# Layer 0 of a two-layer encoder: four k tiles of the query and key projection moved into the first two pieces of the input projection, running sums reloaded into PSUM

## The chip, the cores and the metric

The kernel runs on one NeuronCore of a Trainium2 chip. Its engines work side by side, each on its own queue in order: PE (TensorE, matmuls), DVE (VectorE), ACT (ScalarE), POOL (GpSimd) and SP (SyncE, which here issues nearly all transfers). They meet through semaphores. The metric is the device time of one execution in microseconds, the median of several runs.

## What is computed

A trunk of two layers over 256 positions of width 2048. Each layer makes a conditioned, normalised input h, projects it once with a wide matrix, feeds the columns to four mixers, projects back, and adds a gated feed-forward network:

```python
for l in range(DEPTH):
    mod = (c_act @ w_mod[l] + b_mod[l]).reshape(bn, 6, d)
    ...
    h = layer_norm(x) * (1.0 + scale_m) + shift_m
    proj = h @ w_in[l]
    uv, q_c, kv_c, k_r, sb, sc, sh, ag = jnp.split(proj, IN_SPLITS, axis=-1)
    y_a = gmlp_mixer(uv, ...)
    y_b = mla_mixer(q_c, kv_c, k_r, ...)
    y_c = short_conv_mixer(sb, sc, sh, sconv_w[l])
    y_d = conformer_conv(ag, ...)
    y = jnp.concatenate([y_a, y_b, y_c, y_d], axis=-1) @ w_out[l]
    x = layer_norm(ALPHA * x + (1.0 + gate_m) * y, post_mix_g[l], post_mix_b[l])
    h = layer_norm(x) * (1.0 + scale_f) + shift_f
    x = layer_norm(ALPHA * x + (1.0 + gate_f) * conv_ffn(h, ...), post_ffn_g[l], post_ffn_b[l])
```

All is float32. The modulation `mod` of both layers needs 2 x 2048 x 12288 weights, about 200 MB, for a single vector c.

## The kernel before

**Modulation.** It runs on DVE: each step multiplies a 128-row stripe of `w_mod` (tile `wmod`, one transfer of about 1 MB into one of four raw buffers) by a scalar per partition and adds it to an accumulator (`qacc` for layer 0's first two vectors, `macc` for the rest). A product on PE with a column of ones (`ps_mod`) then sums over partitions. The steps beyond the first two vectors come from a generator, `mods`: `pump` draws from it at a rate per unit of weights, set by the stage (`RATES`), and `STEPS` says how many queued background pieces of the convolution (`convD` taps, a product on ACT and an add on DVE) each unit releases.

**Layer 0's input projection, by pieces.** The first h depends on shift and scale, which take 33 MB of `w_mod`. So `by_pieces` cuts the 16 k tiles of the contraction into five pieces (`PIECES`: 2, 2, 4, 4, 4 tiles). While piece q is multiplied, the modulation columns of piece q + 1 are streamed in, in the shares that `some_mods` names. In each piece the columns of four groups are multiplied in four steps s: a quarter of group D (1024 columns, kept in four PSUM banks throughout), then in `side` one of the groups U, V and E (512 columns, two banks). Six banks of this kind (`acc_tile`) exist, so U, V and E share the two that D leaves. After each piece `side` evacuates them: ACT copies a bank, DVE adds it to a running sum in SBUF (lines 1284 to 1290).

**Two kinds of weights.** In the first four k tiles (`PLAIN_KT`), and for U, V and E up to the last piece, weights are used as plain float32 (`exact`, tile `wexact`); one such product is two rows on PE in the profile. Elsewhere a weight tile `wraw` is split into a high part (`whi`, a cast on ACT) and the rest (`wlo`, a subtraction on DVE), three products each. Exact tiles take the buffers of `whi` and `wlo` in turn, four each, so eight in rotation.

**Behind the pieces** come `mix_d` (starts the convolution: `gluD`), `mix_u` (GELU of U's sums), `mix_v`, then stage B, the 768 columns of query, key-value and rotary key over all 16 k tiles (`group`, eight units of two tiles, all exact, banks `B_c`), with `mix_b` (attention, `kvr` to `yb`) flushed into stage C, the last group of columns; then the output projection. `stream` runs each unit's products one unit after its load.

**Order.** Instructions go to each engine's queue in an order that a scheduler sets at build time; a queue never overtakes. All transfers of weights and of `w_mod` stand in SP's one queue, so that a transfer whose buffer is still in use holds all those behind it.

Of the kernel before, what the change touches and what calls it, by code (L numbers as in the profile page):

```python
# [13 lines left out]
P = 128  # L14
# [18 lines left out]


RATES = [
    dict(B=1.6, C=1.9, out=1.7, first=1.2, up=0.68, down=0.83),
    dict(D=0.8, U=0, V=0, B=0.3, C=0.6, E=0.6, out=0.6, up=0.3, down=0.7),
]

STEPS = [  # L40
    dict(B=2, C=2, up=2),
    dict(U=5, V=5, B=4, C=6, E=6, up=2),
]

# [10 lines left out]
def encoder_kernel(ctx: ExitStack, tc: tile.TileContext, A: dict, consts: bass.AP, out: bass.AP):  # L55
# [23 lines left out]
    def acc_tile(name):  # L79
        return accp.tile([P, 512], F32, tag="acc", name=name)  # L80

    def mm(o, lhsT, rhs, start, stop):
        pe.matmul(o, lhsT, rhs, start=start, stop=stop, skip_group_check=True)  # L83
# [389 lines left out]
        act.copy(hi, src)  # L473
        dve.tensor_tensor(out=lo, in0=src, in1=hi.bitcast(F32), op=ALU.subtract)  # L474

    def group(w, c0, width, name, then, ntm=0, nk=2, hF=None, bg=0, spare=0):

        ncm = (width - 512 * ntm) // P  # L480
        box = {}

        def products(item, u):
            if u == 0:
                box["c"] = [acc_tile(f"{name}_c{i}") for i in range((ncm + 1) // 2)]
                box["t"] = [[acc_tile(f"{name}_t{t}{i}") for i in range(ntm)] for t in range(2)]
                box["h"] = list(hT)
            for part in (range(0, min(4, ncm)), range(4, ncm)):
# [33 lines left out]
        def end():  # L522
            then(box["c"], box["t"])

        return KT // nk, load, products, end, bg

    def group2(w, c0, name, then, bg=0, spare=0):


        nk = 4  # L530
        box = {}

        def products(item, u):
            if u == 0:
                box["c"] = [acc_tile(f"{name}_c{i}") for i in range(4)]
                box["h"] = list(hT)
            for i in range(4):
                for k, (hi, _) in enumerate(item):
                    kt = u * nk + k
                    both = box["h"][kt // 2][2][:, kt % 2, :, :].rearrange("p h t -> p (h t)")  # L540
                    mm(box["c"][i], hi[:, i * P : (i + 1) * P], both, kt == 0, False)
            for i in range(4):
                for k, (_, lo) in enumerate(item):
                    kt = u * nk + k
                    high = box["h"][kt // 2][0][:, kt % 2, :]
                    mm(box["c"][i][:, :S], lo[:, i * P : (i + 1) * P], high, False, kt == KT - 1)

        def load(u):
            return weights(w, u * nk, nk, c0, 512, False, spare if u == 0 else 0)

        return KT // nk, load, products, lambda: then(box["c"]), bg

    def run(g):
        units, load, products, end, bg = g
        for u in range(units):
            stream(lambda: load(u), lambda item, u=u: products(item, u), bg)
        pending.append(end)

# [684 lines left out]
    def by_pieces(l, w_in, hF, between, mix_d, mix_u, mix_v, mix_b, mix_c, mix_e):  # L1243
# [1 line left out]

        hf = lambda kt: hF[kt // 4][:, kt % 4, :]
        accD = [acc_tile(f"D{l}_c{i}") for i in range(4)]
        cols = {"U": C_UV, "V": C_UV + 512, "E": C_SB}

        hT[:] = [None] * (PLAIN_KT // 2) + [act_pair("hT") for _ in range((KT - PLAIN_KT) // 2)]  # L1250
        sums = {}
# [17 lines left out]
                    mm(o, w[:, i * P : (i + 1) * P], x, first and n == 0 and i % 2 == 0, last and n == len(ts) - 1)  # L1269

        def side(g, parts, k0, nkt):
            ps = [acc_tile(f"{g}{l}_{i}") for i in range(2)]
            for kt, part in parts:
                st, sp = kt == k0, kt == k0 + nkt - 1
                if g == "V":
                    ts = terms(kt, part)
                    for t in range(2):
                        for n, (w, x) in enumerate(ts):
                            mm(ps[t], x[:, t * P : (t + 1) * P], w, st and n == 0, sp and n == len(ts) - 1)
                else:  # L1280
                    chan_major(ps, kt, part, range(4), st, sp)
            for i in range(2):
                if k0 == 0:
                    act.copy(sums[g][i], ps[i])
                elif k0 + nkt == KT:
                    dve.tensor_tensor(out=sums[g][i], in0=ps[i], in1=sums[g][i], op=ALU.add)
                else:
                    part = tmp_tile("part")
                    act.copy(part, ps[i])
                    dve.tensor_tensor(out=sums[g][i], in0=part, in1=sums[g][i], op=ALU.add)  # L1290

        first = between(0)[1]
        first()
        for q, (k0, nkt) in enumerate(PIECES):
# [3 lines left out]

            def load(g, kt):

                c0, width = (C_AG, 1024) if g == "D" else (cols[g], 512)
                nk = min(2048 // width, nkt)
                for j, p in enumerate(weights(w_in, kt, nk, c0, width, exact or (g != "D" and q < len(PIECES) - 1))):
                    loaded[(g, kt + j)] = p

# [14 lines left out]
            for s in range(4):  # L1320
# [5 lines left out]
                    ahead[1]()  # L1326
                for kt, h in mine:
                    d_part(kt, h)
                if s < 3:
                    g = "UVE"[s]  # L1330
                    load(g, k0)
                    some_mods((0.5, 0.85, 1.0)[s])
                    side(g, [(kt, loaded[(g, kt)]) for kt in range(k0, k0 + nkt)], k0, nkt)
        mix_d(accD, None)
        mix_u(sums["U"], None)
        mix_v(None, [[x] for x in sums["V"]])
        phase(l, "B")
        run(group(w_in, C_Q, 768, f"B{l}", mix_b, hF=hf, bg=STEPS[l]["B"]))
        phase(l, "C")

        def mix_ce(cps, tps):
# [265 lines left out]
```

## Time and profile before

| what | value |
|---|---|
| median of 3 runs | 2297.42 us (2294.97 to 2298.74) |
| the profiled execution's own time | 2298.88 us |
| its span, first to last instruction | 2297.1 us, mean granted PE clock 0.987 |
| PE busy | 2238.4 us, 97% |
| DVE busy | 1790.7 us, 78% |
| ACT busy | 1071.6 us, 47% |
| moved | 605.21 MB, mean 263 GB/s |

The profile is of one execution. Busy shares are means over stages with different limits, so the views used below cut the span into stretches: layer 0's pieces lie between 29.6 and 188.6 us, stage B up to 235.5, stage C and attention up to 327, where the output projection starts. A row of the timeline merges instructions of one kind: start, length, engine, line, operation, output <- inputs, shapes and count, and in brackets the idle time before it with its releaser. On SP the length is that of issuing, waits included, not that of the transfer.

### The profile page before, as it was taken

The numbers are of one execution on the slowest core, as the hardware profiler recorded it, in microseconds if no ns is written. First come the engines' busy times: TensorE is split into PE (matmuls) and PEld (weight loads), VectorE is DVE, ScalarE is ACT, GpSimd is POOL, SyncE is SP. The second block draws the span as 40 slices with busy tenths as digits, with TensorE's granted clock in tenths as the row PEclk, the third lists the DMA queues.
The fourth block names the chain that finished last, engine by engine and source line by source line (L and its number), as shares of the span: only waits on it lengthen the run. The fifth ranks groups of instructions, "written<-read, shape, count | busy, mean of one in ns | idle before, by whom it ended". The sixth has DMA issues, their size and how long they took to land.

```text
span 2297.1 us, 31478 instructions
## 1 busy us (share of the span) xinstructions
PE 2238.4 (97%) x12387; PEld 1934.1 (84%) x12387; DVE 1790.7 (78%) x2211; ACT 1071.6 (47%) x1597; POOL 34.4 (1%) x65
## 2 busy tenths in 40 slices
PE   6899999999999999999999999999999999999998
PEld 4688886798888888888789999889888888888886
DVE  6878987778888888998977899796676565565676
ACT  2235742335454544544455435545454454454553
POOL 2000000000000000000000000000000000000000
PEclk9899999999999999999999999999999999999999
DMA  9999788777889888898857677875665555555554
GB/s 344 362 340 343 271 321 333 263 278 279 317 303 335 292 326 318 303 354 307 311 186 260 202 238 252 291 260 185 249 243 202 193 178 197 192 193 185 188 195 147
DMA packets 228717, 605.21 MB, mean 263 GB/s; under 512 B 14660, under 2 KB 27188, under 8 KB 210900
## 3 DMA queue, kind: packets, MB, share of 16 engines
q1 hardware_dynamic: 227784, 602.30, 73.7%
q8 instruction: 97, 1.59, 0.3%
q0 software_dynamic: 784, 0.90, 0.1%
q14 instruction: 52, 0.43, 0.0%
HBM read 601.05 MB, written 2.10 MB: 263 GB/s over the span
## 4 chain that ended last, share of the span: by engine, by line
PE 89%; DVE 5%; DMA 3%; issue 1%; ACT 1%; SPq 0%; POOL 0%; DVEq 0%; POOLq 0%; ACTq 0%
PE g_c L83 21%; PE v_c L83 21%; PE d L83 20%; PE o L83 8%; PE D_c L83 4%; PE C_c L83 4%; PE B_c L83 3%; DMA wmod<-in_w_mod_dram 2%; PE U_c L83 1%; DVE wlo L454 1%; PE U L83 1%; PE E L83 1%; PE ps_mod L83 1%; PE E_c L83 1%; DVE qacc L248 1%
## 5 line engine op out<-in xcount | busy, mean ns | idle before, releaser
L453 ACT CAST whi<-wraw 128x1024 fp32r<-128x1024 f32 (+1 forms) x632 | 643.6, 1043 | 780.4 <-PE g_c L83 210.0
L454 DVE TENSOR_TENSOR wlo<-wraw,whi 128x1024 fp32r<-128x1024 f32 (+1 forms) x632 | 750.6, 1214 | 292.2 <-ACT whi L453 278.3
L83 PE MATMUL d<-whi,a 128*128 128x512 f32 x1344 | 390.6, 392 | 0.9 <-ACT whi L453 0.9
L248 DVE SCALAR_TENSOR_TENSOR macc<-wmod,cact,macc 128x2048 f32<-128x2048 f32 (+2 forms) x174 | 353.8, 2033 | 32.3 <-DMA wmod<-in_w_mod_dram 31.7
L83 PE MATMUL v_c<-hT,whi 128*128 128x512 f32 (+1 forms) x1456 | 343.1, 383 | 0.0
L83 PE MATMUL g_c<-hT,whi 128*128 128x512 f32 (+1 forms) x1344 | 313.3, 380 | 0.0
L83 PEld LDWEIGHTS v_c<-hT,whi 128*128 128x128 f32 x1456 | 264.6, 189 | 48.5
L83 PEld LDWEIGHTS d<-whi,a 128*128 128x128 f32 x1344 | 253.2, 189 | 54.6 <-ACT whi L453 2.2
L83 PEld LDWEIGHTS g_c<-hT,whi 128*128 128x128 f32 x1344 | 243.4, 189 | 43.2
L83 PE MATMUL d<-wlo,a 128*128 128x512 f32 x672 | 234.4, 392 | 1.6 <-DVE wlo L454 1.6
L83 PE MATMUL v_c<-hT,wlo 128*128 128x256 f32 x1400 | 190.7, 283 | 0.0
L83 PEld LDWEIGHTS v_c<-hT,wlo 128*128 128x128 f32 x1400 | 183.1, 191 | 6.6
L83 PE MATMUL g_c<-hT,wlo 128*128 128x256 f32 x1280 | 175.8, 283 | 0.0
L83 PEld LDWEIGHTS g_c<-hT,wlo 128*128 128x128 f32 x1280 | 168.2, 191 | 5.9
L83 PEld LDWEIGHTS d<-wlo,a 128*128 128x128 f32 x672 | 127.0, 189 | 30.3 <-DVE wlo L454 3.9
L473 ACT CAST a<-g 128x512 fp32r<-128x512 f32 x132 | 80.8, 619 | 91.0 <-PE d L83 89.3
L83 PE MATMUL o<-whi,a 128*128 128x512 f32 x384 | 112.4, 398 | 0.8 <-ACT whi L453 0.8
L474 DVE TENSOR_TENSOR a<-g,a 128x512 fp32r<-128x512 f32 x132 | 87.7, 685 | 9.5 <-ACT a L473 9.5
L83 PEld LDWEIGHTS o<-whi,a 128*128 128x128 f32 x384 | 73.1, 191 | 17.5 <-ACT whi L453 1.2
L83 PE MATMUL D_c<-hT,whi 128*128 128x256 f32 x432 | 82.0, 290 | 2.8 <-ACT hT L473 2.3
L248 DVE SCALAR_TENSOR_TENSOR qacc<-wmod,cact,qacc 128x1024 f32<-128x1024 f32 (+1 forms) x75 | 80.3, 1070 | 2.6 <-DMA wmod<-in_w_mod_dram 0.5
L1364 DVE SCALAR_TENSOR_TENSOR u<-g,pf,u 128x254 f32<-128x254 f32 (+1 forms) x176 | 73.5, 476 | 3.0 <-ACT u L86 3.0
(371 smaller groups left out, 2603.7 us busy)
## 6 DMA issues: line engine op xcount, KB each, us to landing
wraw<-in_ffn_w_up_dram SPq DMA_DIRECT2D x168, 1024.0 KB, 5.0
wmod<-in_w_mod_dram SPq DMA_DIRECT2D x134, 1024.0 KB, 6.2
wraw<-in_ffn_w_down_dram SPq DMA_DIRECT2D x88, 1024.0 KB, 5.2
wraw<-in_w_in_dram SPq DMA_DIRECT2D x33, 1024.0 KB, 6.9
wmod<-in_w_mod_dram SPq DMA_DIRECT2D x64, 512.0 KB, 9.2
wraw<-in_w_out_dram SPq DMA_DIRECT2D x26, 1024.0 KB, 6.7
wmod<-in_w_mod_dram SPq DMA_DIRECT2D x32, 768.0 KB, 6.6
wexact<-in_w_in_dram SPq DMA_DIRECT2D x46, 512.0 KB, 7.4
```

What stands on the lines that cost most here:

```text
L83: pe.matmul(o, lhsT, rhs, start=start, stop=stop, skip_group_check=True)
L248: i = dve.scalar_tensor_tensor(out=acc, in0=w, scalar=col, in1=acc, op0=ALU.mult, op1=ALU.add)
L453: act.copy(hi[:, :m], r)
L454: i = dve.tensor_tensor(out=lo[:, :m], in0=r, in1=hi[:, :m].bitcast(F32), op=ALU.subtract)
L473: act.copy(hi, src)
L474: dve.tensor_tensor(out=lo, in0=src, in1=hi.bitcast(F32), op=ALU.subtract)
L1364: dve.scalar_tensor_tensor(out=u[:, sh:], in0=x[:, : S - sh], scalar=col(k, j), in1=u[:, sh:], op0=ALU.mult, op1=ALU.add)
```

## The change

- Group B joins the two exact pieces: step s = 1 now runs V and then B (768 columns, three banks one after the other). Its sums lie in two new slots, `sumB0` and `sumB1`. Stage B's `group` starts at k tile 4 (`begun`): its first products find the three sums copied into its banks by ACT.
- `side` works one bank at a time. From the second piece on ACT first copies the running sum back into the bank, the products add to it, and ACT copies the bank out. The adds on DVE are gone.
- In the last piece U's two banks are not copied out: `mix_u` reads them at once, in that step, and no longer behind `mix_d`.
- Three steps of `mods` are drawn in the last piece, one after each of its first three steps. Stage B's rate is 1.634 instead of 1.6 over six units instead of eight, and it releases three background pieces a unit instead of two.

```diff
@@ -33,12 +33,12 @@
 
 
 RATES = [
-    dict(B=1.6, C=1.9, out=1.7, first=1.2, up=0.68, down=0.83),
+    dict(B=1.634, C=1.9, out=1.7, first=1.2, up=0.68, down=0.83),
     dict(D=0.8, U=0, V=0, B=0.3, C=0.6, E=0.6, out=0.6, up=0.3, down=0.7),
 ]
 
 STEPS = [
-    dict(B=2, C=2, up=2),
+    dict(B=3, C=2, up=2),
     dict(U=5, V=5, B=4, C=6, E=6, up=2),
 ]
 
@@ -473,16 +473,21 @@
         act.copy(hi, src)
         dve.tensor_tensor(out=lo, in0=src, in1=hi.bitcast(F32), op=ALU.subtract)
 
-    def group(w, c0, width, name, then, ntm=0, nk=2, hF=None, bg=0, spare=0):
+    def group(w, c0, width, name, then, ntm=0, nk=2, hF=None, bg=0, spare=0, begun=None):
 
 
 
         ncm = (width - 512 * ntm) // P
         box = {}
 
+        skip = 0 if begun is None else PLAIN_KT // nk
+
         def products(item, u):
-            if u == 0:
+            if u == skip:
                 box["c"] = [acc_tile(f"{name}_c{i}") for i in range((ncm + 1) // 2)]
+                if begun is not None:
+                    for bank, part in zip(box["c"], begun):
+                        act.copy(bank, part)
                 box["t"] = [[acc_tile(f"{name}_t{t}{i}") for i in range(ntm)] for t in range(2)]
                 box["h"] = list(hT)
             for part in (range(0, min(4, ncm)), range(4, ncm)):
@@ -522,7 +527,7 @@
         def end():
             then(box["c"], box["t"])
 
-        return KT // nk, load, products, end, bg
+        return range(skip, KT // nk), load, products, end, bg
 
     def group2(w, c0, name, then, bg=0, spare=0):
 
@@ -548,11 +553,11 @@
         def load(u):
             return weights(w, u * nk, nk, c0, 512, False, spare if u == 0 else 0)
 
-        return KT // nk, load, products, lambda: then(box["c"]), bg
+        return range(KT // nk), load, products, lambda: then(box["c"]), bg
 
     def run(g):
         units, load, products, end, bg = g
-        for u in range(units):
+        for u in units:
             stream(lambda: load(u), lambda item, u=u: products(item, u), bg)
         pending.append(end)
 
@@ -1245,7 +1250,7 @@
 
         hf = lambda kt: hF[kt // 4][:, kt % 4, :]
         accD = [acc_tile(f"D{l}_c{i}") for i in range(4)]
-        cols = {"U": C_UV, "V": C_UV + 512, "E": C_SB}
+        cols = {"U": (C_UV, 512), "V": (C_UV + 512, 512), "E": (C_SB, 512), "B": (C_Q, 768)}
 
         hT[:] = [None] * (PLAIN_KT // 2) + [act_pair("hT") for _ in range((KT - PLAIN_KT) // 2)]
         sums = {}
@@ -1269,26 +1274,28 @@
                     mm(o, w[:, i * P : (i + 1) * P], x, first and n == 0 and i % 2 == 0, last and n == len(ts) - 1)
 
         def side(g, parts, k0, nkt):
-            ps = [acc_tile(f"{g}{l}_{i}") for i in range(2)]
-            for kt, part in parts:
-                st, sp = kt == k0, kt == k0 + nkt - 1
-                if g == "V":
-                    ts = terms(kt, part)
-                    for t in range(2):
+            for i, total in enumerate(sums[g]):
+                o = acc_tile(f"{g}{l}_{i}")
+                if k0 > 0:
+                    act.copy(o, total)
+                for kt, part in parts:
+                    st, sp = kt == 0, kt == k0 + nkt - 1
+                    if g == "V":
+                        ts = terms(kt, part)
                         for n, (w, x) in enumerate(ts):
-                            mm(ps[t], x[:, t * P : (t + 1) * P], w, st and n == 0, sp and n == len(ts) - 1)
+                            mm(o, x[:, i * P : (i + 1) * P], w, st and n == 0, sp and n == len(ts) - 1)
+                    else:
+                        chan_major([None] * i + [o], kt, part, (2 * i, 2 * i + 1), st, sp)
+                if g == "U" and k0 + nkt == KT:
+                    u_banks.append(o)
                 else:
-                    chan_major(ps, kt, part, range(4), st, sp)
-            for i in range(2):
-                if k0 == 0:
-                    act.copy(sums[g][i], ps[i])
-                elif k0 + nkt == KT:
-                    dve.tensor_tensor(out=sums[g][i], in0=ps[i], in1=sums[g][i], op=ALU.add)
-                else:
-                    part = tmp_tile("part")
-                    act.copy(part, ps[i])
-                    dve.tensor_tensor(out=sums[g][i], in0=part, in1=sums[g][i], op=ALU.add)
-
+                    act.copy(total, o)
+            if u_banks and g == "U":
+                mix_u(u_banks, None)
+
+        u_banks = []
+        both = [slot("sumB0"), slot("sumB1")]
+        sums["B"] = [both[i // 2][:, (i % 2) * 512 : (i % 2 + 1) * 512] for i in range(3)]
         first = between(0)[1]
         first()
         for q, (k0, nkt) in enumerate(PIECES):
@@ -1298,8 +1305,8 @@
 
             def load(g, kt):
 
-                c0, width = (C_AG, 1024) if g == "D" else (cols[g], 512)
-                nk = min(2048 // width, nkt)
+                c0, width = (C_AG, 1024) if g == "D" else cols[g]
+                nk = min(max(2, 2048 // width), nkt) if exact else min(2048 // width, nkt)
                 for j, p in enumerate(weights(w_in, kt, nk, c0, width, exact or (g != "D" and q < len(PIECES) - 1))):
                     loaded[(g, kt + j)] = p
 
@@ -1326,16 +1333,16 @@
                     ahead[1]()
                 for kt, h in mine:
                     d_part(kt, h)
-                if s < 3:
-                    g = "UVE"[s]
+                for g in ("U", "VB", "E", "")[s] if exact else ("U", "V", "E", "")[s]:
                     load(g, k0)
-                    some_mods((0.5, 0.85, 1.0)[s])
+                    some_mods((0.5, 0.85, 1.0, 1.0)[s])
                     side(g, [(kt, loaded[(g, kt)]) for kt in range(k0, k0 + nkt)], k0, nkt)
+                if k0 + nkt == KT and s < 3:
+                    next(mods)
         mix_d(accD, None)
-        mix_u(sums["U"], None)
         mix_v(None, [[x] for x in sums["V"]])
         phase(l, "B")
-        run(group(w_in, C_Q, 768, f"B{l}", mix_b, hF=hf, bg=STEPS[l]["B"]))
+        run(group(w_in, C_Q, 768, f"B{l}", mix_b, hF=hf, bg=STEPS[l]["B"], begun=sums["B"]))
         phase(l, "C")
 
         def mix_ce(cps, tps):
```

Where the instructions now stand, at three places. First SP's queue behind the last modulation transfers of piece 1 (`wmod` 128x4x256 goes before). `wexact` 128x2x512 is a tile of U, V or E, 128x768 one of B, 128x1024 one of D; `wmod` 128x2x512 is two stripes of 512 columns for piece 2. A wait on PE is a wait for a buffer that products still read, one on DVE for a raw buffer, one on a DMAHW semaphore for the eighth transfer before. Before, from E of piece 0 to U of piece 1:

```order
L431 DMA wexact<-in_w_in_dram 128x2x512 [waits DMAHW0_49]
L431 DMA wexact<-in_w_in_dram 128x1024 [waits DMAHW1_49]
L431 DMA wexact<-in_w_in_dram 128x1024 [waits DMAHW2_49]
L263 DMA wmod<-in_w_mod_dram 128x2x512 [waits DMAHW3_49,DVE_49]
L263 DMA wmod<-in_w_mod_dram 128x2x512 [waits DMAHW4_49]
L263 DMA wmod<-in_w_mod_dram 128x2x512 [waits DMAHW5_49,DVE_49]
L263 DMA wmod<-in_w_mod_dram 128x2x512 [waits DMAHW6_49]
L263 DMA wmod<-in_w_mod_dram 128x2x512 [waits DMAHW7_49,DVE_49]
L263 DMA wmod<-in_w_mod_dram 128x2x512 [waits DMAHW0_49]
L431 DMA wexact<-in_w_in_dram 128x2x512 [waits DMAHW1_49]
```

Now, from B of piece 0 to U of piece 1:

```order
L431 DMA wexact<-in_w_in_dram 128x768 [waits DMAHW0_49]
L431 DMA wexact<-in_w_in_dram 128x768 [waits DMAHW1_49]
L431 DMA wexact<-in_w_in_dram 128x2x512 [waits DMAHW2_49]
L431 DMA wexact<-in_w_in_dram 128x1024 [waits DMAHW3_49]
L431 DMA wexact<-in_w_in_dram 128x1024 [waits DMAHW4_49,PE_49]
L263 DMA wmod<-in_w_mod_dram 128x2x512 [waits DMAHW5_49,DVE_49]
L263 DMA wmod<-in_w_mod_dram 128x2x512 [waits DMAHW6_49]
L263 DMA wmod<-in_w_mod_dram 128x2x512 [waits DMAHW7_49,DVE_49]
L263 DMA wmod<-in_w_mod_dram 128x2x512 [waits DMAHW0_49]
L263 DMA wmod<-in_w_mod_dram 128x2x512 [waits DMAHW1_49,DVE_49]
L263 DMA wmod<-in_w_mod_dram 128x2x512 [waits DMAHW2_49]
L431 DMA wexact<-in_w_in_dram 128x2x512 [waits DMAHW3_49,PE_49]
```

The second D tile and the U tile of piece 1 now wait for PE, which they did not.

Second, DVE's queue in piece 2, from its first modulation step for piece 3 (`qacc`, the add of `sumU` being the running sum of U). Before:

```order
L246 TENSOR_SCALAR qacc<-wmod,cact 128x1024
L248 SCALAR_TENSOR_TENSOR qacc<-wmod,cact,qacc 128x1024 x7
L1290 TENSOR_TENSOR sumU<-part,sumU 128x512 x2
L248 SCALAR_TENSOR_TENSOR qacc<-wmod,cact,qacc 128x1024 x6
L454 TENSOR_TENSOR wlo<-wraw,whi 128x1024
L1290 TENSOR_TENSOR sumV<-part,sumV 128x512
L454 TENSOR_TENSOR wlo<-wraw,whi 128x1024
L1290 TENSOR_TENSOR sumV<-part,sumV 128x512
L248 SCALAR_TENSOR_TENSOR qacc<-wmod,cact,qacc 128x1024 x2
```

Now:

```order
L246 TENSOR_SCALAR qacc<-wmod,cact 128x1024
L248 SCALAR_TENSOR_TENSOR qacc<-wmod,cact,qacc 128x1024
L474 TENSOR_TENSOR hT<-hF_116,hT 128x2x256 x2
L248 SCALAR_TENSOR_TENSOR qacc<-wmod,cact,qacc 128x1024 x12
L454 TENSOR_TENSOR wlo<-wraw,whi 128x1024 x2
L248 SCALAR_TENSOR_TENSOR qacc<-wmod,cact,qacc 128x1024 x2
L454 TENSOR_TENSOR wlo<-wraw,whi 128x1024 x2
```

The adds, each waiting for ACT's copy of a bank that PE has finished, no longer stand between the modulation steps.

Third, DVE's queue from piece 4 to `gluD`, the first work of `mix_d`. Before:

```order
L454 TENSOR_TENSOR wlo<-wraw,whi 128x1024 x2
L246 TENSOR_SCALAR macc<-wmod,cact 128x2048
L454 TENSOR_TENSOR wlo<-wraw,whi 128x1024
L248 SCALAR_TENSOR_TENSOR macc<-wmod,cact,macc 128x2048
L1286 TENSOR_TENSOR sumV<-V_0_1172,sumV 128x512
L1286 TENSOR_TENSOR sumV<-V_1_1173,sumV 128x512
L454 TENSOR_TENSOR wlo<-wraw,whi 128x1024
L248 SCALAR_TENSOR_TENSOR macc<-wmod,cact,macc 128x2048 x2
L1286 TENSOR_TENSOR sumE<-E_0_1244,sumE 128x512
L1286 TENSOR_TENSOR sumE<-E_1_1245,sumE 128x512
L870 TENSOR_TENSOR gluD<-D_c_119,sg 128x512
```

Now:

```order
L474 TENSOR_TENSOR hT<-hF_118,hT 128x2x256 x2
L246 TENSOR_SCALAR macc<-wmod,cact 128x2048
L454 TENSOR_TENSOR wlo<-wraw,whi 128x1024 x3
L248 SCALAR_TENSOR_TENSOR macc<-wmod,cact,macc 128x2048
L454 TENSOR_TENSOR wlo<-wraw,whi 128x1024 x4
L248 SCALAR_TENSOR_TENSOR macc<-wmod,cact,macc 128x2048
L454 TENSOR_TENSOR wlo<-wraw,whi 128x1024
L248 SCALAR_TENSOR_TENSOR macc<-wmod,cact,macc 128x2048 x2
L875 TENSOR_TENSOR gluD<-D_c_119,sg 128x512
```

Five steps of `macc` stand ahead of `gluD` instead of four; behind it, up to the end of attention, there are 30 convolution taps as before and one modulation step less.

## The prediction

> **What bounds it.** I read the busy time by stretches first. Columns: stretch and its length; busy us (instructions) of PE, weight loads, VectorE (DVE), ScalarE (ACT), GpSimd; granted clock, DMA share, GB/s. The first four stretches are pieces 0 to 3 of layer 0's input projection, each from the modulation sums of its piece to those of the next; the fifth is piece 4. The last, from a second answer, goes from the first DVE work of `mix_d` to the end of attention, stages B and most of C.
>
> ```profile
> 29.60:51.60 22.00, 21.91 (x80) 17.61 (x81) 12.09 (x17) 3.95 (x8) 0.00 (x0) 0.81 1.06 373
> 51.60:80.40 28.80, 24.34 (x95) 17.74 (x93) 23.35 (x26) 4.55 (x10) 5.32 (x10) 0.88 0.97 346
> 80.40:120.80 40.40, 35.67 (x178) 29.35 (x177) 32.54 (x33) 11.32 (x18) 0.00 (x0) 0.92 1.01 372
> 120.80:157.50 36.70, 35.16 (x198) 28.94 (x197) 30.03 (x30) 9.85 (x16) 0.00 (x0) 1.00 0.98 355
> 157.50:188.60 31.10, 30.80 (x236) 29.64 (x235) 24.45 (x25) 12.50 (x16) 0.00 (x0) 1.00 0.80 282
> ...
> 190.80:300.80 110.00, 109.37 (x530) 93.86 (x529) 103.00 (x118) 70.29 (x170) 4.36 (x6) 1.00 0.86 314
> ```
>
> Up to 157.5 us the transfers fill the time (346 to 373 GB/s, share about 1) and PE has gaps. From piece 4 on PE is full: 30.80 of 31.10 and 109.37 of 110.00. But in that last stretch DVE is busy 103.00 of 110.00 too. So two limits lie close together where the change takes work away, and the transfers are the limit where it puts work.
>
> **Removed: a quarter of stage B.** The PE timeline of stage B (start, length, operation, count):
>
> ```profile
> 202.62 32.54 PE L83 MATMUL B_c<-hF,wexact 128*128 128x256 f32 x150
> ```
>
> One row costs 32.54 / 150 = 0.217 us. A plain float32 product is two rows, so 16 k tiles by 6 blocks are 192 rows; the change takes 48 of them out of this full stretch: 10.4 us of PE.
>
> **Added: the same rows in pieces 0 and 1**, 24 rows or 5.2 us each, and four weight transfers of 384 KB, 1.57 MB, which at 372 GB/s (piece 2's row) take 4.2 us of a stream that is already full. What counts is when the stream is held. First SP's queue, then PE, then the way of one weight tile from issue to landing in the chain of waits, and the issue row of the smallest transfer, whose last column is its time to landing:
>
> ```profile
> 32.57 3.44 SPq L431 DMA_DIRECT2D wexact<-in_w_in_dram  x3
> 36.11 7.27 SPq L263 DMA_DIRECT2D wmod<-in_w_mod_dram  x6
> 43.80 1.34 SPq L431 DMA_DIRECT2D wexact<-in_w_in_dram  x1
> ```
> ```profile
> 43.87 3.60 PE L83 MATMUL V<-wexact,hF 128*128 128x512 f32 x8
> ...
> 48.17 3.62 PE L83 MATMUL E<-hF,wexact 128*128 128x256 f32 x16
> 51.62 0.95 PE L83 MATMUL ps_mod<-onesR,qacc 128*128 128x1 f32 x8
> 52.43 1.11 PE L83 MATMUL D_c<-hF,wexact 128*128 128x256 f32 x4
> ...
> 75.15 5.38 PE L83 MATMUL E<-hF,wexact 128*128 128x256 f32 x16 [2.04 <-DMA wexact<-in_w_in_dram]
> 80.36 1.84 PE L83 MATMUL ps_mod<-onesR,qacc 128*128 128x1 f32 x16
> ...
> 157.50 1.84 PE L83 MATMUL ps_mod<-onesR,qacc 128*128 128x1 f32 x16
> ```
> ```profile
> 68.00 7.01 DMA wexact<-in_w_in_dram
> ```
> ```profile
> cst<-in_consts_dram SPq DMA_DIRECT2D x1, 64.0 KB, 2.0
> ```
>
> Exact weights rotate through eight buffers. Before, piece 0 used five, so D, D and U of piece 1 went out by 43.8 without a wait. Now piece 0 uses seven. Piece 1's second D tile takes the buffer of piece 0's first, read until V starts at 43.87. Piece 1's U takes that of piece 0's second D tile, whose last product stands behind E and ps_mod: 52.43 + 1.11 plus two transposes, some 53.8, and now 5.2 later, 59. Everything on SP queues behind: six modulation loads after the D tile, and after U the rest of piece 2's modulation, V, B and E. From 43.9 the stream has seven transfers of 0.524 MB, 3.67 MB or 9.9 us; with 2.0 us to the first landing (the small transfer's row) it is dry at 55.8. It restarts at 59 + 2 = 61 with 13 transfers of 0.524 MB and two of 0.393 up to piece 1's E: 7.6 MB, 20.4 us, landing at 81.4. Before, E landed at 68.00 + 7.01 = 75.0. **Delay: 6.4 us.** Before there was one such hole, of two microseconds, when the modulation steps were held:
>
> ```profile
> 56.00:60.00 4.00, 4.00 (x23) 3.56 (x22) 3.89 (x4) 0.00 (x0) 3.31 (x7) 1.00 0.66 185
> ```
>
> **Given back: the running sums.** DVE's in-order queue stood before these adds, with modulation steps, whose raw buffers the stream needs, behind them:
>
> ```profile
> 99.42 0.69 DVE L1290 TENSOR_TENSOR sumU<-part,sumU 128x512 f32<-128x512 f32 x1 [3.24 <-ACT part L1289]
> ...
> 137.43 0.69 DVE L1290 TENSOR_TENSOR sumU<-part,sumU 128x512 f32<-128x512 f32 x1 [2.40 <-ACT part L1289]
> ```
>
> The adds are gone. If pieces 2 and 3 (77.1 us at a mean of 364 GB/s) then flow at 372, they take 75.4: 1.7 us back. So piece 4's sums come 6.4 - 1.7 = **4.7 us late**. Ends: without a hole the bytes cost 4.2, and PE's gaps of 4.7 and 1.5 us in pieces 2 and 3 could all close, -2; with a second hole as long as one piece's B products, 5.2 more, +11.6, keeping the 6.4. I take 4.7, nearest to the rows above.
>
> The reloads go to ACT:
>
> ```profile
> L1289 ACT COPY part<-U x6: 586/586/587, 64.5 to 137.7; 128x512 f32<-128x512 f32 x6
> ```
>
> Evacuating a bank and reloading it take 2 x 0.59 = 1.2 us, behind the other bank's products: 8 rows or 1.7 us in pieces 0 and 1, twice that in 2 and 3, while ACT is busy 3.95 of 22.00 in piece 0. So nothing. There are 30 reloads; bare, they would cost 30 x 0.59 = 17.6 us, and a part of that would show as PE waiting for line 1280. U's GELU in piece 4 holds both banks and adds a table load:
>
> ```profile
> 180.26 1.28 ACT L869 ACT_TABLE_LOAD   x1
> ```
> ```profile
> 171.04 2.88 PE D_c L83 x24
> ```
>
> D's 24 products, 2.88 us in the chain of waits, stand between U's second bank and V on PE; the table load is over by then, and GELU and reload, two ACT passes of some 0.6 us, fit in. The three moved modulation steps (3.1 MB) find the room of piece 4's stream, (372 - 282) x 31.1 = 2.8 MB, and nothing.
>
> **What stage B can give.** PE's need in the last stretch falls from 109.4 to 99.0 us. DVE's falls only by one modulation step, which now stands ahead of `mix_d`:
>
> ```profile
> L248 DVE SCALAR_TENSOR_TENSOR macc<-wmod,cact,macc 128x2048 f32<-128x2048 f32 x12 | 28.1, 2344 | 1.5 <-DMA wmod<-in_w_mod_dram 1.5
> ```
>
> 103.0 - 2.3 = 100.7 us. All 30 conv taps, 21 other modulation steps and the attention arithmetic stay in it, in one queue on which PE's attention products wait. DVE becomes the longer side. What it waited for:
>
> ```profile
> DVE macc L248 <- DMA wmod<-in_w_mod_dram: 2.4, 2, 1.5
> DVE gluD L870 <- ACT sg L869: 1.6, 1, 1.6
> DVE convD L903 <- ACT prodD L902: 1.3, 3, 0.5
> DVE rr L1066 <- POOL rr L114: 0.9, 1, 0.9
> DVE qc L1099 <- PE ps_qr L83: 0.6, 1, 0.6
> DVE rr L1059 <- PE ps_ss L83: 0.5, 1, 0.5
> ```
>
> The last three are steps of one chain and stay, 2.0 us; of the first three, 5.3, I keep a third. 100.7 + 3.5 = 104.2: the stretch gives 110 - 104.2 = **5.8 us, not 10.4**. Ends: with no wait 9.3, with all 7.0 us of them 2.3. Behind attention the C products left on PE are about as many as before, so the rest is only shifted.
>
> **Sum.** -5.8 + 4.7 = -1.1 us on the profiled execution's 2298.9. That execution is 1.5 above the median 2297.4, so I predict **2296.3**.
>
> [...] The row at 75.15 needed 5.38 us for what took 3.62 at 48.17, after a gap of 2.04; the clock in that neighbourhood:
>
> ```profile
> 68.00:72.00 4.00, 4.00 (x6) 1.53 (x6) 3.89 (x4) 0.00 (x0) 0.00 (x0) 0.57 0.93 319
> ```
>
> [...]
>
> **Rivals.** (1) The stream catches up and DVE closes its gaps: the hole is short, piece 4 late by 1.5, the stretch gives 9: -7.5, **2290**. For it: the freed DVE and 6 us of PE gaps; against: eight buffers and the held U. Chance 0.20. (2) Slower: a second hole. Piece 2's U tiles take the buffers of piece 1's V and first B tile; B runs bank by bank, so that tile is free only at B's end, and the stream stands again for up to 5.2 us. Piece 4 is then 11.6 late, +5.8, **2303**; over 0.2% slower from a delay of 10.4 on. For it: the same mechanism as in piece 0; against: SP gets to those tiles about when B ends. Chance 0.17. (3) DVE keeps all its waits: the stretch gives 2.3, +2.4, **2300**. For it: the waits are on chains; against: three were for late data. Chance 0.20. (4) Slow clock: B's 5.2 us in piece 1 stretches as E's row did, 5.38 / 3.62, to 7.7, and PE sets the end of piece 1, 2.5 us later: **2299**. For it: it follows a wait, as E's row did; against: V stands between that wait and it, and after E's row the clock was back at 1.00 (piece 3). Chance 0.08. My forecast keeps 0.35.
>
> **Range.** A measurement here tells about 0.2% from no change, 4.6 us. Faster: (1) and the forecast's edge, 0.30. Slower: (2) and the edges of (3) and (4), 0.20. Within: 0.50. The range reaches from under (1) to (2)'s threshold, 2288.5 to 2302.5.
>
> **What will show it.** Right: U of piece 1 issued at about 59 and a dip in GB/s just before; piece 4's ps_mod near 162 instead of 157.5; DVE without idle from `mix_d` on; PE waiting several microseconds in all for DVE in attention. Wrong: U issued before 50, or ps_mod of piece 4 at 159 or earlier (rival 1), past 168 (rival 2), PE free of waits in stage C (the 10.4 came through), or PE waiting for reloads.

## The result and the profile after

The changed kernel takes 2287.2 us, median of 9 runs (2284.0 to 2296.5), beside 2298.7 for the kernel before in 9 runs of the same session. The ratio is 0.9960, 95% interval 0.9948 to 0.9972: 9 us faster, between 6 and 12. The forecast was 2296.3, within 0.2% of before, and the time lies 1.3 us under the lower end of its range. The profiled execution took 2287.1 us, span 2285.3.

The stretches again: pieces 0 to 3 from modulation sums to modulation sums, piece 4, then the first DVE work of `mix_d` to the end of attention. Columns as in the prediction. Piece 4's row runs up to `gluD` here, which starts at 190.8 us in both profiles; the row of before ended 2.2 us ahead of it, so these two are not to be compared.

```profile
30.30:55.90 25.60, 25.53 (x104) 21.02 (x104) 12.84 (x18) 6.30 (x12) 0.00 (x0) 0.89 1.06 377
55.90:82.80 26.90, 26.51 (x120) 20.81 (x119) 20.20 (x20) 11.68 (x22) 5.08 (x10) 1.00 0.96 349
82.80:121.00 38.20, 35.78 (x177) 29.30 (x176) 27.32 (x25) 14.46 (x24) 0.00 (x0) 0.91 1.05 389
121.00:156.00 35.00, 34.70 (x198) 28.98 (x197) 26.47 (x25) 13.34 (x22) 0.00 (x0) 1.00 1.04 389
156.00:190.80 34.80, 34.80 (x264) 33.42 (x263) 22.92 (x19) 22.87 (x34) 0.00 (x0) 1.00 0.88 300
190.80:292.50 101.70, 99.96 (x476) 85.22 (x475) 99.88 (x118) 68.24 (x166) 3.86 (x6) 0.98 0.86 317
```

Piece 0 is 3.6 us longer than before (25.60 against 22.00): PE was full there, and B's products came on top. Pieces 1 to 3 are shorter, by 1.9, 2.2 and 1.7 us, although piece 1 carries B too. In pieces 2 and 3 the stream now moves 389 GB/s where it moved 372 and 355, and DVE has 5.2 and 3.6 us less to do. The last stretch ends 8.3 us sooner than before.

SP's queue and PE's timeline around piece 1:

```profile
32.78 9.36 SPq L431 DMA_DIRECT2D wexact<-in_w_in_dram  x5
42.24 3.90 SPq L263 DMA_DIRECT2D wmod<-in_w_mod_dram  x6
46.98 0.44 SPq L431 DMA_DIRECT2D wexact<-in_w_in_dram  x1
```
```profile
43.35 3.60 PE L83 MATMUL V<-wexact,hF 128*128 128x512 f32 x8
...
47.21 5.34 PE L83 MATMUL B<-hF,wexact 128*128 128x256 f32 x24
52.39 3.62 PE L83 MATMUL E<-hF,wexact 128*128 128x256 f32 x16
...
57.98 0.70 PE L83 MATMUL D_c<-hF,wexact 128*128 128x256 f32 x2
...
70.38 3.67 PE L83 MATMUL V<-wexact,hF 128*128 128x512 f32 x8 [0.39 <-DMA wexact<-in_w_in_dram]
74.03 5.47 PE L83 MATMUL B<-hF,wexact 128*128 128x256 f32 x24
79.34 3.62 PE L83 MATMUL E<-hF,wexact 128*128 128x256 f32 x16
```

U's tile of piece 1 was issued at 46.98, not at about 59. That is the moment when piece 0's V products end (43.35 + 3.60 = 46.95), not the end of D's second tile (57.98 + 0.70). The hole that the forecast built on that buffer is not there. The stream does have a hole at nearly that place, as it had one before the change. In 58 to 62 us it moves 145 GB/s. The rows around it, and what SP stood for:

```profile
56.00:60.00 4.00, 4.00 (x24) 3.15 (x23) 2.50 (x7) 1.92 (x5) 1.77 (x4) 1.00 0.71 255
60.00:64.00 4.00, 4.00 (x21) 3.51 (x20) 3.89 (x4) 0.00 (x0) 3.31 (x7) 1.00 0.88 279
```
```profile
SPq L263 <- DVE pf L142: 9.0, 1, 9.0
```

(Total of the waits in us, their number, the longest.) It is the modulation loads that stand here, for DVE, whose queue waits 5.4 us for piece 1's modulation values with the steps behind. Reckoned against 388 GB/s from windows of 1 us, before lost 2.0 us of stream at this place, e1 (below) 1.6, after 2.5. And V and E of piece 1 take 3.67 and 3.62 us where E took 5.38 before.

What DVE waited for in the pieces, before and after:

```profile
DVE hF L1477 <- ACT mod L86: 12.0, 4, 8.4
DVE sumU L1290 <- ACT part L1289: 7.5, 5, 3.2
DVE wlo L454 <- ACT whi L453: 4.8, 3, 2.6
DVE sumE L1290 <- ACT part L1289: 3.2, 3, 1.7
```
```profile
DVE wlo L454 <- ACT whi L453: 14.5, 5, 5.2
DVE hF L1484 <- ACT mod L86: 9.4, 4, 5.4
DVE qacc L248 <- DMA wmod<-in_w_mod_dram: 7.9, 5, 2.9
```

Before, DVE stood 10.7 us for copies of finished banks. After, these waits are gone, and DVE stands longer for casts of weights (14.5 us against 4.8) and for the stream itself (7.9 us for `wmod`), which it did not in the rows of before.

### The profile page after: what moved, and what is told of

Its sections match the earlier page's. It is cut to its first block, busy times and chain, and to the rows that moved or that the text cites. A ratio compares the mean times of both kernels' runs of the same rounds, so it can differ in the third digit from the quotient of the medians.

```text
span 2285.3 us, 31502 instructions
## 1 busy us (share of the span) xinstructions
PE 2233.5 (98%) x12387; PEld 1929.9 (84%) x12387; DVE 1773.9 (78%) x2187; ACT 1095.1 (48%) x1638; POOL 33.7 (1%) x65
## 4 chain that ended last, share of the span: by engine, by line
PE 53%; DVE 4%; DMA 1%; issue 1%; ACT 1%; POOL 0%; DVEq 0%; POOLq 0%; ACTq 0%
PE d L83 20%; PE v_c L83 12%; PE g_c L83 11%; PE o L83 2%; PE D_c L83 2%; PE C_c L83 2%; PE U_c L83 1%; DVE wlo L454 1%; DVE convD L886 1%; PE E_c L83 1%; DMA wmod<-in_w_mod_dram 1%; DMA wraw<-in_w_out_dram 1%; DVE macc L248 0%; PE ps_mod L83 0%; PE ps_xT L592 0%
## 5 line engine op out<-in xcount | busy, mean ns | idle before, releaser
L83 PEld LDWEIGHTS D_c<-hT,whi 128*128 128x128 f32 x432 | 69.8, 197 | 4.8 <-ACT hT L473 1.7
```

## The experiments

All ratios are against the kernel before, with the 95% interval. The two middle columns come from each kernel's profiled execution: from the first ps_mod sums (piece 0's start) to those of piece 4, and from there to the first product of the output projection. "us less" is (1 - ratio) x 2297.

| kernel | pieces 0 to 3 | piece 4 to first `o` | ratio | us less |
|---|---|---|---|---|
| before | 127.9 | 169.2 | 1 | |
| after | 125.7 | 160.8 | 0.9960 (0.9948 to 0.9972) | 9.2 |
| e1 reload only | 121.1 | 166.8 | 0.9963 (0.9950 to 0.9977) | 8.5 |
| e2 move only | 131.3 | 164.3 | 1.0007 (0.9999 to 1.0016) | -1.6 |
| e3 remove only | 121.7 | 161.3 | 0.9949 (0.9937 to 0.9962) | 11.7 |
| e4 add only | 127.0 | 167.1 | 0.9989 (0.9980 to 0.9998) | 2.5 |
| e5 adds, no wait | (115.9) | 166.8 | 0.9960 (0.9945 to 0.9975) | 9.2 |
| e6 piece 1 only | 124.7 | 163.8 | 0.9969 (0.9958 to 0.9981) | 7.1 |
| e7 fewer taps | 127.6 | 164.1 | 0.9979 (0.9970 to 0.9988) | 4.8 |
| e8 own buffers | 125.4 | 160.9 | 0.9960 (0.9947 to 0.9973) | 9.2 |
| e9 adds behind copy | 132.1 | 167.0 | 1.0003 (0.9993 to 1.0013) | -0.7 |
| e10 adds in place | 120.7 | 166.9 | 0.9962 (0.9948 to 0.9975) | 8.7 |
| e11 banks in turn | 129.1 | 168.3 | 0.9996 (0.9987 to 1.0006) | 0.9 |
| e12 steps later | 127.0 | 166.7 | 0.9987 (0.9978 to 0.9995) | 3.0 |

The five kernels whose early pieces do the same work (after, e4, e7, e8, e12) spread from 125.4 to 127.6 in their single profiles, so a figure of that column is good to about 1 us. A profiled execution as a whole can lie several microseconds off its kernel's median (that of e7 4.9 above, that of e3 4.5 below), so the columns and the ratios need not agree.

### Which half of the change pays

**e1**: the new `side` and U's GELU from the banks, put into the kernel before; B whole in its stage.

```diff
-            ps = [acc_tile(f"{g}{l}_{i}") for i in range(2)]
...
+            for i, total in enumerate(sums[g]):
+                o = acc_tile(f"{g}{l}_{i}")
+                if k0 > 0:
+                    act.copy(o, total)
...
-        mix_u(sums["U"], None)
```

> Only the running sums change: U, V and E are reloaded into PSUM and U's GELU reads the banks; B stays whole in its own stage and no modulation step is moved. 24 vector adds of about 0.69 us go (16.6 us of DVE). Theory A (the stream of pieces 2 and 3 was held by DVE, and half or more of the gain is this): 3 to 5 us less than before, piece 4's sums 3 us earlier, GB/s of pieces 2 and 3 near 389 as after. Theory B (the gain is the 48 rows that left stage B): 0 to 2 us less. Forecast's figure for this part: 1.7 us less.

**e2**: B's move alone; the sums go over DVE as before.

```diff
+            if g == "B":
+                for i in range(3):
+                    o = acc_tile(f"{g}{l}_{i}")
...
+                        part = tmp_tile("part")
+                        act.copy(part, o)
+                        dve.tensor_tensor(out=sums[g][i], in0=part, in1=sums[g][i], op=ALU.add)
```

> Only B moves (with its three modulation steps); the sums of U, V and E, and B's in piece 1, are added on DVE as before, and U's GELU waits for its sum. Theory A: the stream stays held by DVE, pieces end 3 to 5 us later than before, stage B and attention give 8: 3 to 5 us less than before. Theory B: 8 to 10 us less, as after. Forecast's figure (hole of 6.4 in the stream, stretch gives 5.8): within 1 us of before.

The reload alone brings 8.5 us. The move alone brings nothing: its pieces take 3.4 us more than before, the rest 4.9 less. Both of my theories had the shares wrong: A gave the reload 3 to 5 us, B 0 to 2. The stretches of e1, pieces 1 to 3:

```profile
51.10:77.30 26.20, 22.67 (x94) 16.70 (x94) 21.13 (x21) 8.14 (x16) 5.61 (x10) 0.93 1.00 364
77.30:115.30 38.00, 34.53 (x177) 27.91 (x176) 27.53 (x25) 14.57 (x24) 0.00 (x0) 0.96 1.05 389
115.30:150.30 35.00, 34.70 (x198) 28.98 (x197) 26.46 (x25) 13.23 (x22) 0.00 (x0) 1.00 1.04 390
```

The 389 GB/s of pieces 2 and 3 are there without B's move. Each of the three pieces is 1.7 to 2.6 us shorter than before, 6.8 in all with piece 0.

### The price of B's early rows and what they are worth

**e3** leaves k tiles 0 to 3 of the query and key projection out (first edit); **e4** computes them early and again in stage B (second edit).

```diff
-                for g in ("U", "VB", "E", "")[s] if exact else ("U", "V", "E", "")[s]:
+                for g in ("U", "V", "E", "")[s]:
...
-                    st, sp = kt == 0, kt == KT - 1
+                    st, sp = kt == skip * nk, kt == KT - 1
```
```diff
-    dict(B=1.634, C=1.9, out=1.7, first=1.2, up=0.68, down=0.83),
+    dict(B=1.225, C=1.9, out=1.7, first=1.2, up=0.68, down=0.83),
...
-        run(group(w_in, C_Q, 768, f"B{l}", mix_b, hF=hf, bg=STEPS[l]["B"], begun=sums["B"]))
+        run(group(w_in, C_Q, 768, f"B{l}", mix_b, hF=hf, bg=STEPS[l]["B"]))
```

> As after, but k tiles 0 to 3 of the query and key projection are not computed at all: no loads and no products of B in pieces 0 and 1, no reload into stage B's banks. What it lacks against after is the price of the added work. If the added work is free beside the stream: same as after, 10 to 12 us less than before. If it costs its PE time in piece 0 (full before) and nothing in piece 1: 5 us less than after, 15 to 16 less than before. If each of its 10.7 us of products counts: 20 less than before. If DVE is the longer side of stage B to attention (forecast): no more than 2 us less than after whatever the pieces give.

> As after, but stage B computes all 16 k tiles and never uses the early sums: the added work without the removed one (modulation steps per stage kept: three early, the rest at 1.225 a unit). The difference to after is what the 48 rows are worth in stage B. If PE sets that stretch: 10 us more than after (within 1.5 us of before). If DVE sets it, as the forecast had it: 6 us more than after, 4 to 6 us less than before.

With sums reloaded, the pieces take 121.1 and 121.7 us without B's early rows (e1, e3) and 125.4 to 127.6, on average 126.5, with them: the early rows cost 5.1 us. They come back as 6.0 us behind piece 4 (166.8 in e1 to 160.8). By the medians after and e1 can't be told apart; e4 and after can, by 6.7 us. By its median e3 is where it was expected if the added rows were free (11.7 us less), but its interval, 8.7 to 14.5 us, does not tell that case from the next. By the profiles the rows are not free, and they don't cost all of their 10.8 us of products either.

Most of that price can be put down to bytes. Over pieces 0 to 3 e1 moves 46.1 MB at a mean of 381 GB/s, after 47.5 MB at 378: the stream runs equally full, and the 1.4 MB more are 3.6 us of the 4.6 between the two profiles. The rest is about what the hole near 60 us grew, 0.9. PE has 8.8 us more to do there. No run adds the bytes without the products, so this is a reckoning, not a test.

**e6**: only k tiles 2 and 3, in piece 1; stage B skips that unit. Two modulation steps come early instead of three, and stage B releases two background pieces a unit.

```diff
+        todo = [u for u in range(KT // nk) if begun is None or u != 1]
...
-                for g in ("U", "VB", "E", "")[s] if exact else ("U", "V", "E", "")[s]:
+                for g in ("U", "VB", "E", "")[s] if q == 1 else ("U", "V", "E", "")[s]:
```

> As after, but only k tiles 2 and 3 of B go ahead, into piece 1, whose PE had gaps; piece 0, full before, is left as it was; two modulation steps early instead of three, and before's two background steps a unit in stage B. If the price of the move is piece 0's PE time (pieces 0 to 3 of after end 5.7 us later than with reloaded sums alone, 3.6 of them in piece 0): pieces end 1 to 3 us later than there, stage B gives about 3 to 5, 10 to 12 us less than before. If the price is bytes in the stream or buffers: half of after's, so 8 to 9 us less than before.

Its pieces take 124.7 us, 3.6 more than e1 for half of the rows, and the rest 163.8, 3.0 less. Leaving PE's full piece 0 alone did not make the move pay, so PE's time in piece 0 is not the whole price.

**e8**: B's four tiles in buffers of their own.

```diff
-                for j, p in enumerate(weights(w_in, kt, nk, c0, width, exact or (g != "D" and q < len(PIECES) - 1))):
+                for j, p in enumerate(weights(w_in, kt, nk, c0, width, exact or (g != "D" and q < len(PIECES) - 1), 2 * (g == "B"))):
```

> As after, but the four weight tiles of B have buffers of their own, so the eight exact buffers serve D, U, V and E alone, as before the change. Forecast's mechanism (B's tiles hold the stream through the rotation): SP's wait before piece 1's second D tile goes, pieces end 3 to 5 us earlier than after, 3 to 5 us less than after. If the price is PE's 5.3 us in piece 0: within 1 us of after.

125.4 us and 9.2 less: as after. In after SP waits 4.8 us for a buffer ahead of piece 1's second D tile, issued at 41.82; in e8 this wait is gone, the tile is out by 37.14, and nothing comes of it; the hole at 58 to 62 us is there too (101 GB/s). The rotation of the eight buffers costs nothing here.

### Why the reload pays: DVE's time or DVE's wait

**e5** gave e1 the removed adds back, on an idle tile:

```diff
                     act.copy(total, o)
+                if k0 > 0:
+                    dve.tensor_tensor(out=dummy[:, 512:], in0=dummy[:, :512], in1=dummy[:, 512:], op=ALU.add)
```

> The kernel with reloaded sums and B unmoved (8 us less than before), to which DVE gets 24 adds of the removed ones' shape back at their places, on a tile that nobody reads and with nothing to wait for. If what the removal brought was DVE's time as such (24 x 0.69 = 16.6 us, of which DVE is the engine that releases the raw buffers): most of the gain is lost, 0 to 3 us less than before. If it was the wait of DVE's queue for ScalarE's copy in front of each add (3.24 and 2.40 us in two rows of before): the gain stays, 6 to 8 us less than before.

It says nothing of the question. The row of the idle tile (count, shortest, median and longest in ns, first and last start) shows that all 24 were run ahead of piece 1, mostly before piece 0's sums, which came at 34.4 us instead of 29.2 in e1; hence the bracketed 115.9:

```profile
L1289 DVE TENSOR_TENSOR dummy<-dummy x24: 675/683/693, 3.8 to 46.5; 128x512 f32<-128x512 f32 x24
```

Two kernels with the adds held in place settle it, and a third tries PE's order. **e9**'s adds read the sum that ScalarE has just copied; **e10**'s touch the idle tile alone and are ordered behind the modulation step ahead of them; **e11** is the kernel before with its side products written bank by bank. The edits in that order:

```diff
+                    dve.tensor_tensor(out=dummy[:, 512:], in0=total, in1=dummy[:, 512:], op=ALU.add)
```
```diff
+                    d = dve.tensor_tensor(out=dummy[:, 512:], in0=dummy[:, :512], in1=dummy[:, 512:], op=ALU.add)
+                    tc.add_manual_dep(d.ins, last_step[0], order_dep, reason="after the steps ahead of it")
```
```diff
-            ps = [acc_tile(f"{g}{l}_{i}") for i in range(2)]
-            for kt, part in parts:
+            ps = []
+            for i in range(2):
+                o = acc_tile(f"{g}{l}_{i}")
+                ps.append(o)
+                for kt, part in parts:
```

> Reloaded sums, B unmoved (8.5 us less than before), and DVE gets 22 adds of 0.69 us back, each reading the sum that ScalarE has just copied out of its bank, into a tile that nobody reads: DVE's time and its wait for the copy are back, with PE's order and the reloads as they are. If either of the two made the 8 us: 0 to 3 us less than before, piece 4's sums at 155 to 158. If the gain came from PE's order (one bank after the other) or from the U sum read from PSUM: still 7 to 9 less, piece 4 at 150.

> The same, but the 22 adds read and write the idle tile alone, and each is ordered on DVE behind the modulation step written ahead of it: DVE's time is back within the pieces, the wait for ScalarE's copy is not. (In the earlier try without that order they ran before 46.5 us, ahead of the pieces, so that run says nothing of DVE's time in them.) If the wait held the stream: 6 to 8 us less than before, piece 4 at 150 to 152. If DVE's time did: as with the wait, 0 to 3 less, piece 4 at 155 to 158.

> The kernel before, with only the order of the side products changed: the k tiles of one bank, then those of the other, with the copies and DVE adds as before. If PE's order made the gain: 6 to 8 us less than before. If DVE's adds or their waits held the stream: within 2 us of before.

DVE's queue in piece 2 of e9, then of e10:

```profile
87.64 6.57 DVE L248 SCALAR_TENSOR_TENSOR qacc<-wmod,cact,qacc 128x1024 f32<-128x1024 f32 x5
97.53 0.69 DVE L1289 TENSOR_TENSOR dummy<-sumU,dummy 128x512 f32<-128x512 f32 x1 [3.32 <-ACT sumU L1287]
98.14 2.60 DVE L248 SCALAR_TENSOR_TENSOR qacc<-wmod,cact,qacc 128x1024 f32<-128x1024 f32 x2
```
```profile
90.89 2.60 DVE L250 SCALAR_TENSOR_TENSOR qacc<-wmod,cact,qacc 128x1024 f32<-128x1024 f32 x2 [0.34 <-DMA wmod<-in_w_mod_dram]
93.41 0.68 DVE L1292 TENSOR_TENSOR dummy<-dummy 128x512 f32<-128x512 f32 x1
94.01 1.28 DVE L250 SCALAR_TENSOR_TENSOR qacc<-wmod,cact,qacc 128x1024 f32<-128x1024 f32 x1
```

The same 22 adds, 15.2 us of DVE, cost nothing in e10 (8.7 us less than before, pieces 120.7) and the whole gain in e9 (none, pieces 132.1). DVE had the time; what it lacked was a queue that moves. In e9 the modulation steps stop at 94.21 (87.64 + 6.57); the add ahead of the next one waits 3.32 us for a copy, and that step runs right behind it, at 98.14, without a wait of its own. Until then its raw buffer is not free, and SP's queue stands behind it: SP issues nothing from 95.28 to 100.77, and in 102 to 106 us the stream of e9 falls to 281 GB/s (before: 249) where that of e10 holds 386. All of e10's adds ran between 65.2 and 149.6 us, within pieces 1 to 3, those of piece 4 too, so DVE had no less to do there than in e9. PE's order is not it (e11: 0.9 us).

### What stage B's rows are worth, and what eats the rest

After lost 10.4 us of PE work behind piece 4 and got 6.0 of time, against e1. From piece 4's sums to the first `o`, e1 and then after:

```profile
150.30:317.10 166.80, 166.79 (x905) 147.69 (x904) 139.93 (x155) 99.36 (x210) 4.27 (x7) 1.00 0.86 315
156.00:316.80 160.80, 158.91 (x857) 139.28 (x856) 138.79 (x157) 104.42 (x218) 4.56 (x7) 0.99 0.85 310
```

PE never idles there in e1, nor in e4 (167.04 of 167.10): it sets the time of this stretch as long as B is whole. In after PE is busy 7.9 us less, not 10.4, because some rows ran at a lower clock (the 24 of C at 227.69 took 6.90 us, which at 0.217 each are 5.2; the clock was 0.66 in 226 to 230 us), and it idles 1.9. PE's rows at B's norm in after, and in e1:

```profile
222.36 0.95 PE L83 MATMUL ps_ss<-onesR,sqB 128*128 128x1 f32 x8
223.17 1.97 PE L83 MATMUL C_c<-hF,wexact 128*128 128x256 f32 x8
226.12 1.70 PE L83 MATMUL ps_ss<-onesR,sqB 128*128 128x1 f32 x12 [0.98 <-ACT sqB L1045]
227.69 6.90 PE L83 MATMUL C_c<-hF,wexact 128*128 128x256 f32 x24
235.34 0.67 PE L83 MATMUL ps_rkv<-dgB,onesR 128*128 128x256 f32 x2 [0.76 <-DVE dgB L1074]
...
237.00 5.45 PE L83 MATMUL ps_qn<-qg,wq 128*128 128x256 f32 x24
```
```profile
227.00 0.89 PE L83 MATMUL ps_ss<-onesR,sqB 128*128 128x1 f32 x6
...
234.97 5.34 PE L83 MATMUL ps_qn<-qg,wq 128*128 128x256 f32 x24
```

From the norm's first sum to the first query product e1 needs 8.0 us with 18 rows of C between, after 14.6 with 32. The 14 rows more are 3.0 us at 0.217; the other 3.6 are the two waits and a clock that fell. **e7** and **e12** (edits in that order) asked which engine is behind:

```diff
-    dict(B=3, C=2, up=2),
+    dict(B=2, C=3, up=2),
```
```diff
-    dict(B=1.634, C=1.9, out=1.7, first=1.2, up=0.68, down=0.83),
+    dict(B=1.2, C=1.9, out=1.917, first=1.2, up=0.68, down=0.83),
```

> As after, with two background steps a unit in stage B instead of three and three instead of two in stage C: 12 instead of 18 of the convolution's steps on ScalarE and DVE lie ahead of B's norm. In after PE waited 1.0 and 0.8 us there and the clock fell to 0.66; B's end to the first query product took 14.6 us with 32 rows of C in it, against 8.0 with 18 rows when B was whole. If DVE's and ScalarE's backlog holds the norm (DVE is the longer side of stage B): no waits there, 2 to 4 us less than after, 12 to 14 less than before. If the convolution's end is what counts (ps_var behind attention): same or up to 3 us more than after.

> As after, but stage B takes 1.2 modulation steps a unit instead of 1.634 and the output projection 1.917 instead of 1.7: two or three steps (2.1 us of DVE each) go from the stretch in which DVE was full (99.88 of 101.70 us to the end of attention) to one in which it was not (41.08 of 52.50). Of the 10.4 us of PE that left stage B, after got 6.0 against the kernel with reloaded sums alone; 1.8 were waits at B's norm, where the clock fell too. If the number of DVE's steps in that stretch is what cost the rest: the waits before ps_ss and ps_rkv go and the end comes 2 to 4 us earlier than in after, 11 to 13 less than before. If they come from the norm's own chain: same as after, 9 to 10 less than before.

Both came out worse than after, by 4.4 and 6.2 us, and neither theory of e12 holds. In e7 the wait before ps_ss stays (1.0 us), and the taps put into stage C make PE wait 2.3 us for `qc`. e4's 6.7 us more than after is the figure that was expected if DVE set the stretch, but PE is the engine that is full in e4. e12 shows what holds PE at the norm. Its ScalarE and PE there:

```profile
220.45 0.38 ACT L1045 ACTIVATE sqB<-B_c 128x256 f32<-128x256 f32 x1 [1.31 <-PE B_c L83]
220.83 12.52 ACT L907 ACTIVATE prodD<-gluD,pm 128x246 f32<-128x246 f32 x32
233.25 0.89 ACT L1045 ACTIVATE sqB<-B_c 128x256 f32<-128x256 f32 x3
```
```profile
222.98 5.43 PE L83 MATMUL C_c<-hF,wexact 128*128 128x256 f32 x24
233.66 4.00 PE L83 MATMUL ps_ss<-onesR,sqB 128*128 128x1 f32 x18 [5.26 <-ACT sqB L1045]
```

With fewer modulation steps between them the convolution's steps came forward, and 32 of their ScalarE products, 12.52 us, stand between the norm's first square and the next. After has 8 of them at that place:

```profile
221.67 0.66 ACT L1045 ACTIVATE sqB<-B_c 128x256 f32<-128x256 f32 x2
222.57 3.23 ACT L907 ACTIVATE prodD<-gluD,pm 128x246 f32<-128x246 f32 x8 [0.24 <-DVE convD L908]
225.71 0.36 ACT L1045 ACTIVATE sqB<-B_c 128x256 f32<-128x256 f32 x1
```

So what after loses at the norm, it loses first to ScalarE's queue. No kernel tried here has the squares ahead of the convolution's products, so what that would bring stays open. None of those that compute everything is faster than after beyond the intervals.

## Where the prediction was right and where it failed, step by step

- **Removed, 10.4 us of PE**: as forecast; 144 rows of B are left in stage B.
- **Delay of 6.4 us from held buffers**: the cause was wrong. U of piece 1 was issued at 46.98 instead of 59, and e8 shows that the rotation costs nothing. That the size was near is luck: the early rows cost 5.1 us against the same kernel without them, of which piece 0 shows 3.7 (21.9 in e1, 25.6 in after). The reckoning above gives 3.6 of it to bytes, close to the forecast's other end, 4.2 without a hole; e6 says that it is not PE's time in piece 0 alone. No run tests the division.
- **Given back by the running sums, 1.7 us: the step that failed.** The mechanism was the one named, DVE's in-order queue with modulation steps behind waiting adds. Its size was 6.8 us in the pieces (e1 against before), and 2.4 more behind piece 4. Those 2.4 are not the adds: e9, which has them back, keeps 167.0. In before PE idles 1.8 us there, in e1 not at all; which part of the edit does that is open. I had let two pieces rise to 372 GB/s, the best row of pieces 1 to 3; they rose to 389, and piece 1 gained too. That 372 had been held by the same queue (249 GB/s in 102 to 106 us, behind the add that waits 3.24), so it was no measure of the stream. The term went wrong at one choice: the wait was priced by a rate that contained it.
- **Stage B gives 5.8, not 10.4**: 6.0 (e1 to after), and 8.3 against before in the stretch that the forecast named, with the reload's part in it. The size was near, the reason at most half right. DVE is nearly full there (99.88 of 101.70), but PE is as full (99.96) and waits for DVE only 0.8 us; it waits 1.0 us for ScalarE's squares, and the clock falls (0.66 in 226 to 230 us). The forecast had no wait of PE for ScalarE there. Its sum also has a slip: 2.0 us and a third of 5.3 are 3.8, not 3.5, and would give 5.5.
- **Reloads for nothing**: right; no product of after waits for line 1280. **Three early steps for nothing**: right as far as seen. DVE stands 4.4 us for one of their transfers ahead of `gluD`, but piece 4 is full of PE, 34.80 of 34.80, and e4, which has the early steps and the whole of B, takes 167.1 us behind piece 4's sums where e1 takes 166.8. They were not tried alone.
- **Sum**: -6.5 (pieces without early rows, 121.4 on average, against 127.9) + 5.1 - 2.4 - 6.0 = -9.8 us, and the first `o` product comes 9.9 earlier (316.8 against 326.7).
- **Rivals**: (1), 2290, came nearest by its figure, not by its path. It let piece 4's sums come 1.5 us late and the stretch behind them give 9; they came 2.2 early (125.7 us after piece 0's, against 127.9), and the rest gave 8.4. (2) and (3) did not occur. (4) went the other way: B fills the gap and the clock stays at 1.00.

## What to carry to other kernels

In pieces 2 and 3 of before DVE was busy four fifths of the time (32.54 of 40.40 us and 30.03 of 36.70) and still held the stream, because adds in its queue waited up to 3.24 us for ScalarE: look for rows with a releaser in the middle of a run of buffer-freeing steps, and price the wait, not the instruction's time. A transfer rate read from a stretch that such a wait holds is no ceiling: the 372 GB/s became 389. And work moved into gaps is paid where it lands: here the early rows cost 5.1 us in the pieces, and the move bought nothing that the medians can tell, while the small edit beside it made the gain (e1, 8.5 us).

## What the runs showed of the hardware

Behind a gap of 1.92 us the granted clock fell from 1.00 to 0.50. e1's V in piece 1 and the windows of that place:

```profile
66.98 5.37 PE L83 MATMUL V<-wexact,hF 128*128 128x512 f32 x8 [1.92 <-DMA wexact<-in_w_in_dram]
```
```profile
66.00:68.00 2.00, 1.02 (x3) 0.57 (x4) 1.96 (x2) 0.30 (x1) 0.00 (x0) 1.00 1.05 402
68.00:70.00 2.00, 2.00 (x4) 0.83 (x3) 1.79 (x3) 0.24 (x1) 0.00 (x0) 0.50 1.05 390
70.00:72.00 2.00, 2.00 (x4) 0.63 (x2) 1.96 (x2) 0.94 (x2) 0.00 (x0) 0.65 1.05 387
```

In after the gap is 0.39 and the clock 1.00 in 70 to 74 us, and in e1 a gap of 1.40 us ahead of E left E at 3.69 us, beside 3.62 in after, with the clock at 1.00 in 74 to 78. But at after's norm 0.98 us was followed by 0.50 in 228 to 230 us, with one-column products (`ps_ss`) right behind it and, eight rows of C earlier, ahead of it: in these runs the length of the gap alone did not decide. In e12's gap of 5.26 us the clock fell some 3.7 us after PE's last product, an estimate from the mean of 0.57 in 232 to 233 us, and stayed at half for about 10 us:

```profile
240.00:242.00 2.00, 2.00 (x6) 1.55 (x6) 1.09 (x5) 0.00 (x0) 1.05 (x1) 0.50 1.10 414
242.00:244.00 2.00, 2.00 (x10) 1.73 (x9) 0.70 (x1) 0.88 (x2) 0.00 (x0) 0.90 0.93 373
```

PE was busy again from 233.66 on. The first 4.00 us of that are one-column products (`ps_ss`); from C's first row at 237.52 it took some 5 us until the clock rose (0.50 in 240 to 242, 0.90 in 242 to 244). No run here tells what part the one-column products had in that.
